# Float16 parts in the key and value product and in most of layer 1's output product, and modulation weights read by half tiles

## The chip, the cores and the metric

The kernel runs on one core of a Trainium2 chip, in one launch. The metric is the device time in microseconds (us), the median of several runs. A measurement is told from no change at about 0.2%.

## What is computed

A two-layer diffusion transformer block stack on 256 image tokens and 256 context tokens of width 2048, with branches 4096 wide. Layer 0 mixes with a Fourier transform, layer 1 with windowed attention that also sees the context; the context itself is only needed as far as layer 1's keys and values. Cut to what matters here:

```python
for i in range(2):
    shift, scale, gate = split(silu(c) @ ada_w[i] + ada_b[i], 3)         # modulation; its own for the context
    h  = rmsnorm(x,  norm_g[i]) * (1 + scale)   + shift
    hc = rmsnorm(xc, norm_g[i]) * (1 + scale_c) + shift_c
    if i == 0:                                   # Fourier branch, image and context
        u, z = split(h @ w_in, 2);  y = mix(fft2(u).real) * silu(z)
    else:                                        # attention branch, image only
        q, k, v, z = split(h @ w_in, [4096, 512, 512, 4096])
        kc, vc     = split(hc @ w_in[:, 4096:5120], 2)
        y = attend_with_sink(rope(q), [rope(k), kc], [v, vc], sink, mask) * silu(z)
    x = x + gate * (y @ w_out[i])                # layer 0: xc too
return rmsnorm(x, final_g)
```

Inputs and outputs are float32.

## The kernel before

Matmuls of float32 accuracy are made of three matmuls on two parts (`mm3`): each operand is cast to a high part on ScalarE (ACT) and the rest is its low part, one subtraction on VectorE (DVE); high x high, high x low and low x high are added up in PSUM. There are two kinds of parts. `half_split` makes fp32r parts (lines 66 and 67). `split16` makes float16 parts (lines 137 and 138); there the operand is scaled first by a power of two that follows from a bound of its size, and the result is scaled back when PSUM is read. Such a bound needs the operand's sum of squares ahead of its first use, so the weights are read once more for it: `scan_loads` brings pieces of w_out of layer 0 (`wo0`), `scan_sums` squares them on ACT with a running sum.

```python
def split16(t, i, up):
    w = wsp.tile([P, 2, 1024], F16, tag="ws", name="wf")
    src = t[:, i * 1024 : (i + 1) * 1024]
    last_cast[0] = S.activation(w[:, 0], src, AF.Copy, scale=up).ins
    last_sub[0] = V.scalar_tensor_tensor(w[:, 1], src, up, w[:, 0], op0=ALU.mult, op1=ALU.subtract).ins
```

Weights arrive as 1 MB tiles on SyncE's queue (SP) into `raw`, three buffers. Their parts lie in `ws`, six buffers of 4 KB per partition: an fp32r half takes two of them (high and low), a float16 half takes one. `act` is a pool of 33 buffers of 2 KB for everything else. PSUM has eight banks, each of 512 float32 columns. Each engine works through its instructions in the order that the program lists them, and this order is a scheduler's, from priorities and the `issue_after` contexts in the code.

The stages that matter, with the times of the profile:

- About 310 to 840 us: layer 0's branch; its z product has float16 parts, and DVE works off "jobs" of modulation beside it (`ada_jobs`): a tile of the modulation weights `adw` is multiplied by silu(c) and summed (line 796).
- About 840 to 1002 us: layer 0's output product `wo0`, 32 steps (two sweeps of 16, `kg`), each 24 matmuls of 512 columns. Float16 parts except in the last two steps of a sweep. Here the modulation jobs go on (`ada_rate` of them in step i), now from 1 MB tiles in `raw`; before this stage they read half tiles, `zr` on SP and `wa` on the queue of GpSimd (POOL), the latter into a `ws` buffer. At the end the residual is taken out of PSUM (`evac0`, line 971).
- About 1002 to 1092 us: the key and value product `wkv`. The normalised, modulated input of layer 1 is made per k tile, 128 features each, as fp32r parts for image (`hx1`) and context (`hc1`) by lines 1107, 1108 and 1111. The loop over 8 weight tiles x 2 k x 4 token blocks x 2 (keys, values) fills all eight PSUM banks; then lines 1132 to 1142 read them (a copy and an absolute value of the values, the rotated keys).
- About 1092 to 1600 us: the products for q and z in units, with attention of 32 head blocks between them, and the first column block of layer 1's output product (`w1_next`, `o1_step`, weights `wo1a`). `hx1` serves q and z too. The attention output `y1` is split by `y_split` into fp32r parts `yh`: k under 16 in buffers "h1", 16 to 23 in "act", 24 to 31 in "ys".
- About 1600 us to the end: the rest of the first column block, then `wo1b` (two column blocks, 16 weight tiles of 2 k, 24 matmuls each) and `wo1c` (the last block), all in fp32r parts with `yh` as the stationary side; `evac` multiplies by the gate (`gbc`) and adds the residual, `finish` normalises and stores.

Of the kernel before, what the change touches and what calls it, by code (L numbers as in the profile page):

```python
# [10 lines left out]
F32 = mybir.dt.float32  # L11
F32R = mybir.dt.float32r
# [5 lines left out]
P = 128  # L18
# [14 lines left out]
def tile_dit(ctx: ExitStack, tc: tile.TileContext, a: dict, out: bass.AP):  # L33
# [591 lines left out]
    def h_bound():  # L625
        m = adap.tile([P, 2], F32, name="hm")
        V.tensor_reduce(m[:, 0:1], gs0.rearrange("p k s -> p (k s)"), axis=AX.X, op=ALU.max, apply_absolute_value=True)
        V.tensor_reduce(m[:, 1:2], sh0.rearrange("p k s -> p (k s)"), axis=AX.X, op=ALU.max, apply_absolute_value=True)
        V.scalar_tensor_tensor(m[:, 0:1], m[:, 0:1], 46.0, m[:, 1:2], op0=ALU.mult, op1=ALU.add)
        return as_b(m[:, 0:1])  # L630
# [8 lines left out]
    for g in range(G):  # L639
# [6 lines left out]
        if g == 13:  # L646
            with tc.issue_after(evacs[g - 2][1]), tc.issue_after(evacs[g - 2][0]):
                hb = h_bound()
# [120 lines left out]
    def ada_jobs():  # L769
        for pieces in ((0,), (1, 2, 3)):  # L770
            for kh in range(2):
# [9 lines left out]
                if True:  # L781
                    for i, fg in order:
                        for f in range(2):
                            q = slice(f * 1024, f * 1024 + 1024)
                            if f == 0 and not out0[0]:
                                wf = adat.tile([P, 1024], F32, tag="zr", name="zr", bufs=2)
                                nc.sync.dma_start(wf, a["adw"][i, kh, fg][:, q])
                            elif not out0[0]:
                                wf = wsp.tile([P, 1024], F32, tag="ws", name="wa")
                                nc.gpsimd.dma_start(wf, a["adw"][i, kh, fg][:, q])  # L790
                            else:
                                if f == 0:
                                    w = raw(a["adw"][i, kh, fg])
                                wf = w[:, q]
# [17 lines left out]
    scans, pend = iter(range(64)), []  # L812

    def scan_sums():
        while pend:
            t, j = pend.pop(0)
            S.activation(t, t, AF.Square, accum_out=scn[:, j : j + 1])

    def scan_loads(n):
        for j in [next(scans) for _ in range(n)]:  # L820
            for q in range(2):
# [3 lines left out]
                pend.append((t, j * 2 + q - 64 * (j >= 40)))  # L825
# [20 lines left out]
    with tc.tile_pool(name="yp", reuse_waits="tile", bufs=32) as ypool:  # L846
# [142 lines left out]
        ada_rate = {**{i: 2 for i in (*range(6, 10), *range(17, 25))}, **{i: 0 for i in (14, 15, 16, 29, 30, 31)}}  # L989
        for i in range(32):  # L990
# [5 lines left out]
            if sw == 0:  # L996
                with tc.issue_after(last_cast[0]):
                    scan_sums()
                scan_loads({6: 1, 7: 1, 8: 1, 9: 1}.get(i, 2) if i < 14 else 0)
# [33 lines left out]

    x1d = dram.tile([2, P, D], F32, name="x1d")
# [46 lines left out]
    def roped(dst, src, tb, pool, tag="rt", eng=V):  # L1081
        t2 = pool.tile([P, 512], F32, tag=tag, name="rt")
        sv = src.rearrange("p (h d) -> p h d", d=64)
        eng.tensor_tensor(dst.rearrange("p (h d) -> p h d", d=64), sv, rope[:, 0, tb, :].unsqueeze(1).broadcast_to([P, 8, 64]), op=ALU.mult)
        s4 = src.rearrange("p (h a t i) -> p h a t i", a=2, t=2, i=16)
        t4 = t2.rearrange("p (h a t i) -> p h a t i", a=2, t=2, i=16)
        sn = rope[:, 1, tb, :].rearrange("p (a t i) -> p a t i", a=2, t=2)
# [4 lines left out]
    with tc.tile_pool(name="h1", reuse_waits="tile", bufs=16) as h1p:  # L1092
# [4 lines left out]
        with tc.tile_pool(name="kvp", reuse_waits="tile", bufs=2) as kvp:  # L1097
            hc1 = []
# [561 lines left out]
```

## Time and profile before

| | |
|---|---|
| median of 3 runs | 1773.9 us (1770.9 to 1774.79) |
| the profiled execution | 1775.4 us |
| its span, first to last instruction | 1773.6 us |
| granted TensorE clock, mean | 0.998 |
| busy: TensorE, DVE, ACT, POOL | 1738.5, 1393.7, 1060.4, 294.8 us |
| moved by DMA | 438.74 MB, 247 GB/s on the mean |

The engines in the profile's lines are PE (TensorE's matmuls), PEld (its weight loads), DVE, ACT, POOL and SP. "L145", "L146" and "L147" are the three matmuls of `mm3`; "L66" and "L67" the two halves of a split; a line out of a helper stands for all its callers, so the tiles' names tell the stage. In a line of instructions, "out<-in" is followed by partitions x elements and type; "x" is the number of them, then busy us and the mean ns of one, then the engine's idle time ahead of them and what ended it. In the timeline the first two columns are start and duration in us. A matmul's own duration there overlaps the next one's, so its pace is read from start to start. In the lines on DMA stand the size and the median time from issue to landing.

### The profile page before, as it was taken

How to read it: one execution, taken by the hardware profiler on the slowest of the kernel's cores; microseconds unless marked ns; L12 is line 12 of the kernel's file. 1: busy time of each engine (PE TensorE's matmuls, PEld its weight loads, DVE VectorE, ACT ScalarE, POOL GpSimd, SP SyncE). 2: the span in 40 equal slices, each digit the busy share in tenths (PEclk: the TensorE clock that was granted, in tenths of full speed). 3: DMA queues.
4: the chain of work that ended last, by engine and by line, in shares of the span. 5: the costliest groups of instructions: out<-in, count | busy, mean ns of one | idle time of the engine just before them, and what ended most of it. 6: DMA issues, size and time to landing. Idle time of an engine off the chain costs nothing.

```text
span 1773.6 us, 26403 instructions
## 1 busy us (share of the span) xinstructions
PE 1738.5 (98%) x9517; PEld 1221.7 (69%) x9517; DVE 1393.7 (79%) x2401; ACT 1060.4 (60%) x1989; POOL 294.8 (17%) x368
## 2 busy tenths in 40 slices
PE   6999999999999999999999999999999999999997
PEld 4679999644444444446444888788888888887886
DVE  5779888797777788876885744899999999996455
ACT  5545556477777745553122534787888888885343
POOL 0002111212222132000000000412302230233010
PEclk9999999999999999999999999999999999999999
DMA  9998999778998889865775323588888888887543
GB/s 393 417 346 252 282 264 262 291 285 318 329 306 316 314 293 349 324 249 181 288 297 187 120 95 119 166 207 200 223 205 211 214 214 211 208 212 248 191 166 143
DMA packets 220962, 438.74 MB, mean 247 GB/s; under 512 B 154720, under 2 KB 155120, under 8 KB 189088
## 3 DMA queue, kind: packets, MB, share of 16 engines
q1 hardware_dynamic: 182784, 351.85, 60.6%
q0 software_dynamic: 33904, 78.25, 14.8%
q10 hardware_dynamic: 4144, 6.95, 1.2%
q8 instruction: 75, 1.23, 0.3%
q14 instruction: 55, 0.45, 0.1%
HBM read 391.91 MB, written 12.59 MB: 228 GB/s over the span
## 4 chain that ended last, share of the span: by engine, by line
PE 90%; DVE 4%; DMA 3%; ACT 2%; issue 1%; POOL 0%; ACTq 0%; POOLq 0%; SPq 0%; DVEq 0%
PE ps L145 24%; PE ps L147 24%; PE ps L146 24%; PE ps L1324 6%; PE ps L1326 3%; PE ps L1395 1%; PE ps L1360 1%; PE ps L1361 1%; PE ps L1396 1%; DMA ft<-f 1%; PE ps L286 1%; DMA raw<-in_awp 1%; DVE wl L67 1%; ACT act L864 0%; ACT wf L137 0%
## 5 line engine op out<-in xcount | busy, mean ns | idle before, releaser
L67 DVE TENSOR_TENSOR wl<-raw,wh 128x1024 fp32r<-128x1024 f32 x213 | 281.1, 1324 | 145.5 <-ACT wh L66 129.2
L66 ACT CAST wh<-raw 128x1024 fp32r<-128x1024 f32 x213 | 222.4, 1045 | 178.4 <-PE ps L146 149.7
L146 PE MATMUL ps<-act,wf 128*128 128x512 f16 x512 | 194.0, 379 | 0.0
L147 PE MATMUL ps<-act,wf 128*128 128x512 f16 x512 | 191.1, 379 | 0.0
L145 PE MATMUL ps<-act,wf 128*128 128x512 f16 x512 | 189.8, 379 | 0.6 <-ACT wf L137 0.3
L1324 PE MATMUL ps<-h,wh 128*128 128x512 f32 x512 | 184.8, 396 | 0.0
L147 PEld LDWEIGHTS <-wf 128*128 128x128 f16 x960 | 93.9, 98 | 113.3
L145 PEld LDWEIGHTS <-wf 128*128 128x128 f16 x960 | 93.7, 98 | 113.4 <-ACT wf L137 4.3
L145 PE MATMUL ps<-y,wf 128*128 128x512 f16 x448 | 169.5, 379 | 0.9 <-ACT wf L137 0.9
L146 PE MATMUL ps<-y,wf 128*128 128x512 f16 x448 | 169.8, 379 | 0.0
L146 PEld LDWEIGHTS <-wf 128*128 128x128 f16 x960 | 93.9, 98 | 109.0
L147 PE MATMUL ps<-y,wf 128*128 128x512 f16 x448 | 165.6, 379 | 0.0
L137 ACT ACTIVATE wf<-raw,nrm 128x1024 f16<-128x1024 f32 x56 | 61.2, 1140 | 153.2 <-DMA raw<-in_wo 131.4
L1326 PE MATMUL ps<-h,wl 128*128 128x256 f32 x512 | 138.6, 281 | 0.0
L146 PE MATMUL ps<-wl,h 128*128 128x512 f32 x320 | 126.7, 396 | 0.0
L147 PE MATMUL ps<-wh,h 128*128 128x512 f32 x320 | 125.3, 395 | 0.0
L145 PE MATMUL ps<-wh,h 128*128 128x512 f32 x320 | 124.0, 402 | 0.0
L1378 DVE SCALAR_TENSOR_TENSOR f<-p,sm,f 128x512 f16<-128x512 f32 x128 | 107.4, 859 | 8.6 <-ACT f L1377 8.3
L138 DVE SCALAR_TENSOR_TENSOR wf<-raw,tn,wf 128x1024 f16<-128x1024 f32 x64 | 79.8, 1282 | 42.6 <-ACT wf L137 42.6
L1365 ACT ACTIVATE p<-ps,mx 128x512 f32<-128x512 f32 x128 | 87.9, 688 | 37.2 <-DVE mx L1362 30.8
L1324 PEld LDWEIGHTS ps<-h,wh 128*128 128x128 f32 x512 | 96.2, 188 | 18.9
L1377 ACT ACTIVATE f<-p,sm 128x512 f16<-128x512 f32 x128 | 87.6, 717 | 31.6 <-DMA ft<-f 12.5
(394 smaller groups left out, 4450.2 us busy)
## 6 DMA issues: line engine op xcount, KB each, us to landing
raw<-in_wz SPq DMA_DIRECT2D x64, 1024.0 KB, 5.5
raw<-in_adw SPq DMA_DIRECT2D x38, 1024.0 KB, 6.0
raw<-in_awp SPq DMA_DIRECT2D x32, 1024.0 KB, 13.1
act<-in_wo POOLq DMA_DIRECT2D x128, 256.0 KB, 7.4
raw<-in_wo SPq DMA_DIRECT2D x32, 1024.0 KB, 6.6
raw<-in_wq SPq DMA_DIRECT2D x32, 1024.0 KB, 5.1
raw<-in_wu SPq DMA_DIRECT2D x32, 1016.0 KB, 6.9
raw<-in_wo1b SPq DMA_DIRECT2D x16, 1024.0 KB, 4.9
```

Source lines behind the costliest of these rows:

```text
L66: last_cast[0] = S.copy(h, src).ins
L67: last_sub[0] = eng.tensor_tensor(l, src, h.bitcast(F32), op=ALU.subtract).ins
L137: last_cast[0] = S.activation(w[:, 0], src, AF.Copy, scale=up).ins
L138: last_sub[0] = V.scalar_tensor_tensor(w[:, 1], src, up, w[:, 0], op0=ALU.mult, op1=ALU.subtract).ins
L145: PE.matmul(o, wh, xh, start=start, stop=False)
L146: PE.matmul(o, wh, xl, start=False, stop=False)
L147: return PE.matmul(o, wl, xh, start=False, stop=stop).ins
L1324: PE.matmul(o[0], wh[:, q], hx1[k], start=k == 0, stop=k == KT - 1)
L1326: PE.matmul(o[0][:, 0:N], wl[:, q], hx1[k][:, 0:N], start=False, stop=False)
L1365: S.activation(pt[tb], so[tb], AF.Exp, bias=mx[:, tb : tb + 1], scale=-1.0, accum_out=sm[:, tb : tb + 1])
L1377: S.activation(f[:, 0:512], pt[tb], AF.Copy, scale=sm[:, tb : tb + 1])
L1378: V.scalar_tensor_tensor(f[:, 512:1024], pt[tb], sm[:, tb : tb + 1], f[:, 0:512], op0=ALU.mult, op1=ALU.subtract)
```

## The change

- **Key and value product.** Weights and input become float16 parts. The input is made as scaled float16 parts `hz` (lines 1156, 1158 and 1160 of the changed kernel); since q and z still want fp32r parts, `make_hx1` makes these once more for the image, beside the product (lines 1190 to 1192). Keys and values are scaled back as PSUM is read: the rotation uses a scaled table `ropek`, other copies take a scale.
- **The scales.** `h1_bound` and `h1_scale` work out the input's and the weights' scale at the end of `wo0`, with one trip through DRAM (`hbd`) that brings all partitions' values to each. The sums of squares come from a scan over `wkv`, 14 tiles of `wo1b` and 7 of `wo1c`: 22 half pieces as 44 tiles of 256 KB in steps 10 to 29 of `wo0` (`scan_loads1`, `w_rate`, ACT's squares in line 829), 36 half pieces of 512 KB during the key and value product (`loads2`, line 1184, four buffers `pz`; `sums2`, 28 squares on ACT in line 1177, 8 on DVE in line 1179).
- **Layer 1's output product.** In 28 of 32 k steps of `wo1b` and `wo1c` both sides are float16 parts; `y_sums` squares the attention output on ACT during attention, `out_scale` makes the scales at its end, `y_half` makes y's float16 parts, and `gbc` carries the scale back. The last four k stay fp32r, with scaled weights (`w_scaled`). `wo1a` stays fp32r; `y_split` puts k under 24 in "h1" buffers.
- **Modulation.** The jobs in `wo0` read half tiles (`zr` and `wa`) as the earlier ones do, and `ada_rate` changes in steps 25 and 28.

The core of the diff:

```diff
-                            if f == 0 and not out0[0]:
+                            if f == 0:
                                 wf = adat.tile([P, 1024], F32, tag="zr", name="zr", bufs=2)
                                 nc.sync.dma_start(wf, a["adw"][i, kh, fg][:, q])
-                            elif not out0[0]:
+                            else:
                                 wf = wsp.tile([P, 1024], F32, tag="ws", name="wa")
                                 nc.gpsimd.dma_start(wf, a["adw"][i, kh, fg][:, q])
...
+    def scan_loads1(n):
+        for j in [next(scans1) for _ in range(n)]:
+            for q in range(2):
+                t = act()
+                c = (j % 2 * 2 + q) * 512
+                nc.gpsimd.dma_start(t, wst[j // 2][:, c : c + 512])
...
-        ada_rate = {**{i: 2 for i in (*range(6, 10), *range(17, 25))}, **{i: 0 for i in (14, 15, 16, 29, 30, 31)}}
+        ada_rate = {**{i: 2 for i in (*range(6, 10), *range(17, 26))}, **{i: 0 for i in (14, 15, 16, 28, 29, 30, 31)}}
+        w_rate = {**{i: 1 for i in (10, 14, *range(17, 26), 29)}, **{i: 2 for i in (15, 16, 26, 27, 28)}}
+        def h1_bound():
+            m, c = h_bound(gs1, sh1, False), tiny(F32, 4, "t4")
...
+            nc.gpsimd.dma_start(hbd, c[:, 0:2])
+            hb1.append(act())
+            nc.gpsimd.dma_start(hb1[0][:, 0:N], hbd.rearrange("(o p) c -> o (p c)", o=1).broadcast_to([P, N]))
...
             elif i == 31:
+                with tc.issue_after(last_sub[0]):
+                    h1_scale()
                 wr = raw(a["wkv"][0])
-                w0 = half_split(wr, 0)
+                w0 = split16(wr, 0, upk)
+            if i == 28:
+                with tc.issue_after(last_sub[0]):
+                    h1_bound()
...
+                    h, l = (z2[:, s * 512 + c : s * 512 + c + N] for c in (0, N))
+                    V.scalar_tensor_tensor(t[:, q], x1[k][:, q], gsz[:, k, s : s + 1], r_bc1[:, q] if k else r_ps[s], op0=ALU.mult, op1=ALU.mult)
+                        a_ = S.activation(h, t[:, q], AF.Identity, bias=shz[:, k, s : s + 1]).ins
+                        e = V.scalar_tensor_tensor(l, t[:, q], shz[:, k, s : s + 1], h, op0=ALU.add, op1=ALU.subtract).ins
...
+            def sums2(act_only):
+                for n in range(len(pend)):
+                    t, c = pend.pop(0)
+                    if n % 5 < 3 or act_only:
+                        S.activation(t, t, AF.Square, accum_out=c)
+                    else:
+                        V.tensor_tensor_reduce(t, t, t, 1.0, 0.0, ALU.mult, ALU.add, c)
+            def loads2(n):
+                for j in [next(scans1) for _ in range(n)]:
+                    t = kvp.tile([P, 1024], F32, tag="pz", name="pz", bufs=4)
+                    nc.gpsimd.dma_start(t, wst[j // 2][:, j % 2 * 1024 : j % 2 * 1024 + 1024])
+            def make_hx1(k):
+                V.scalar_tensor_tensor(t, x1[k][:, 0:N], gs1[:, k, 0:1], r_bc1[:, 0:N], op0=ALU.mult, op1=ALU.mult)
+                S.activation(hx[:, 0:N], t, AF.Identity, bias=sh1[:, k, 0:1])
+                V.scalar_tensor_tensor(hx[:, N : 2 * N], t, sh1[:, k, 0:1], hx[:, 0:N].bitcast(F32), op0=ALU.add, op1=ALU.subtract)
...
             for kg in range(8):
-                    w = ws_split(raw(a["wkv"][kg])) if kg else [w0, half_split(wr, 1)]
+                    w = [split16(wr, i, upk) if kg or i else w0 for i in range(2)]
+                with tc.issue_after(last_cast[0]), tc.issue_after(ends[min(kg * 4 + 3, 15)][0]):
+                    sums2(kg < 3)
+                with tc.issue_after(pow_end[0]):
+                    loads2((6, 6, 6, 6, 6, 6, 0, 0)[kg])
...
+                    for k in range(kg * 3 - 3, min(kg * 3, KT)) if kg else ():
+                        make_hx1(k)
...
-                            mm3(o[tb][kv], h[:, c : c + P], h[:, N + c : N + c + P], wh[:, q], wl[:, q], k == 0, k == KT - 1)
+                            mm3(o[tb][kv], hz[k][:, c : c + P], hz[k][:, N + c : N + c + P], wh[:, q], wl[:, q], k == 0, k == KT - 1)
...
+            def y_sums(n, i):
+                    S.activation(act(), y1[j], AF.Square, accum_out=yq[:, j : j + 1])
+            def y_half(j):
+                t = h1p.tile([P, 1024], F16, tag="h1", name="yf", bufs=16)
+                S.activation(t[:, 0:512], y1[j], AF.Copy, scale=uy)
+                V.scalar_tensor_tensor(t[:, 512:1024], y1[j], uy, t[:, 0:512], op0=ALU.mult, op1=ALU.subtract)
...
+            S.activation(gbc[:, 512:], gbc[:, 512:], AF.Copy, scale=dn1)
...
-                w = ws_split(raw(a["wo1b"][kg]))
+                t = raw(a["wo1b"][kg])
+                w = [split16(t, i, uw) if kg < 14 else w_scaled(t, i) for i in range(2)]
+                if kg + 3 < 14:
+                        y_half(kg + 3)
...
-                            mm3(o[tb][c], yh[k][:, tb * P : (tb + 1) * P], yh[k][:, N + tb * P : N + (tb + 1) * P], wh[:, q], wl[:, q], k == 0, k == NB - 1)
+                            mm3(o[tb][c], *(t[:, tb * P : (tb + 1) * P] for t in y_parts(k)), wh[:, q], wl[:, q], k == 0, k == NB - 1)
```

More of the change, by code (lines that the diff above doesn't have):

```diff
@@ L1031, in tile_dit @@
                     evac0(sw * 8 + b, o[b])
+    V.tensor_reduce(yq[:, 16:17], scn[:, 4:16], axis=AX.X, op=ALU.add)
     x1d = dram.tile([2, P, D], F32, name="x1d")
@@ L1448, in tile_dit, with x2_load @@
             nc.gpsimd.dma_start(gbc, gated.broadcast_to([P, D]))
-            x2 = []
-            for tb in range(2):
-                x2.append([act() for _ in range(4)])
-                for c in range(4):
+            x2 = [[], []]
+            def x2_load(c):
+                for tb in range(2):
+                    x2[tb].append(act())
                     nc.gpsimd.dma_start(x2[tb][c], x1d[tb, :, c * 512 : (c + 1) * 512])
+            x2_load(0)
             fg = fp.tile([P, D], F32, name="fg")
```

160 lines of the change are left out of this document (117 added, 43 removed).

## Prediction

> **What bounds the kernel now.** I read the page first, for the shares and the chain.
>
> ```profile
> span 1773.6 us, 26403 instructions
> PE 1738.5 (98%) x9517; PEld 1221.7 (69%) x9517; DVE 1393.7 (79%) x2401; ACT 1060.4 (60%) x1989; POOL 294.8 (17%) x368
> PE 90%; DVE 4%; DMA 3%; ACT 2%; issue 1%; POOL 0%; ACTq 0%; POOLq 0%; SPq 0%; DVEq 0%
> ```
>
> TensorE (PE) is busy 98% of the span and carries 90% of the chain that ended last. So what counts is how many matmuls there are and how far apart they start, not what the other engines do, as long as they keep up. Next came the table by windows, for the stages that the change touches: the output product of layer 0 (842 to 975), the key and value product (1020 to 1064), attention (1140, 1550) and the output product of layer 1 (1641 to 1729).
>
> ```profile
> core 0: us, PE busy (x) PEld busy (x) DVE busy (x) ACT busy (x) POOL busy (x), PEclk, DMA share, GB/s
> 842.46:887.00 44.54, 44.54 (x208) 20.16 (x207) 38.44 (x60) 8.76 (x8) 0.00 (x0) 1.00 0.76 289
> 887.00:931.00 44.00, 44.00 (x205) 19.95 (x204) 39.14 (x59) 9.49 (x9) 0.00 (x0) 1.00 0.77 296
> 1020.00:1064.00 44.00, 44.00 (x190) 35.44 (x189) 21.64 (x39) 14.27 (x25) 0.00 (x0) 1.00 0.27 96
> 1140.00:1186.00 46.00, 43.86 (x246) 36.85 (x245) 42.28 (x75) 38.16 (x76) 14.68 (x10) 1.00 0.75 186
> 1550.00:1596.00 46.00, 46.00 (x245) 37.76 (x244) 44.23 (x82) 40.93 (x90) 16.28 (x16) 1.00 0.82 215
> 1641.00:1685.00 44.00, 44.00 (x192) 35.63 (x191) 19.04 (x17) 16.84 (x16) 0.00 (x0) 1.00 0.55 191
> 1685.00:1729.00 44.00, 44.00 (x191) 35.61 (x190) 25.44 (x24) 19.08 (x24) 4.77 (x3) 1.00 0.48 167
> ```
>
> PE is full at the whole granted clock in the products, while VectorE (DVE) and ScalarE (ACT) are half idle in the key and value product (21.64 and 14.27 of 44 us) and at the end. They are nearly full in attention (DVE 44.23 of 46). Last I read PE's own timeline and the chain, for the pace of one matmul.
>
> ```profile
> 1013.40 0.40 PE L145 MATMUL ps<-wh,h 128*128 128x512 f32 x1
> ...
> 1015.97 0.40 PE L147 MATMUL ps<-wh,h 128*128 128x512 f32 x1
> 839.35 0.38 PE L147 MATMUL ps<-y,wf 128*128 128x512 f16 x1
> ...
> 841.94 0.38 PE L147 MATMUL ps<-y,wf 128*128 128x512 f16 x1
> ```
>
> ```profile
> 1630.83 0.93 PE ps L145 x4
> 1633.63 0.93 PE ps L145 x4
> ...
> 1675.63 0.91 PE ps L145 x4
> 1678.35 0.91 PE ps L145 x4
> ```
>
> Key and value product, fp32r parts: 11 steps in 2.57 us, 233.6 ns apart. Layer 0's output product, float16 parts: 12 steps in 2.59 us, 215.8 ns. The chain through layer 1's output product shows one k step of 12 matmuls each 2.80 us (233.3 ns) and, further on, each 2.72 us (226.7 ns); the second pace goes with the eight steps k = 16 to 23 whose attention parts lie in "act" buffers. So fp32r costs 11 to 18 ns more for each matmul. The weight loads differ in the same sense:
>
> ```profile
> L146 PEld LDWEIGHTS ps<-wl,ys 128*128 128x128 f32 x192 | 36.1, 188 | 8.5 <-DVE wl L67 0.2
> L147 PEld LDWEIGHTS <-wf 128*128 128x128 f16 x960 | 93.9, 98 | 113.3
> ```
>
> The Trainium skill (TensorE: Matmul & The Clock Gate, "Wait — 56ns, not 53.3ns?") gives a warm 512-column matmul 215.7 ns from start to start, whatever the type. By that rule the change removes nothing from PE. The float16 rows agree with it (215.8); the fp32r rows do not (233.6), and the measurement decides.
>
> **What the change removes.** Key and value product: 16 k x 4 token blocks x 2 halves x 3 = 384 matmuls x (233.6 - 215.8) = 6.8 us. Layer 1's second and third column blocks: 28 of 32 steps, 12 and 6 matmuls each, 18 together. Twenty of those steps run at 233.3 now: 20 x 18 x 17.5 = 6.3 us; eight at 226.7: 8 x 18 x 10.9 = 1.6 us. The first column block stays fp32r, and its eight "act" steps move to the "h1" buffers: 8 x 6 x 6.6 ns = 0.3 us lost, if the pace goes with the buffer. Sum: 6.8 + 6.3 + 1.6 - 0.3 = **14.4 us**. PE is full there, so this counts one to one if the feeding keeps up.
>
> **What it adds, and where that lies.** Prices:
>
> ```profile
> L645 ACT ACTIVATE pz<-pz 128x1024 f32<-128x1024 f32 x12 | 12.8, 1065 | 5.5 <-DMA pz<-in_wz 5.5
> L817 ACT ACTIVATE act<-act 128x512 f32<-128x512 f32 x128 | 78.6, 615 | 0.0
> L817 ACT ACTIVATION_READ_ACCUMULATOR act<-act 128x1 f32 x128 | 24.0, 188 | 0.0
> L796 DVE CUSTOM_DVE_ANT_0 wa<-wa,cb 128x1024 f32<-128x1024 f32 x26 | 31.8, 1223 | 0.7
> L1107 DVE SCALAR_TENSOR_TENSOR ht<-act,gs 128x256 f32<-128x256 f32 x30 | 12.7, 479 | 0.3 <-ACT act L1113 0.3
> L1108 ACT ACTIVATE h<-ht,sh 128x256 fp32r<-128x256 f32 x16 | 8.1, 507 | 7.5 <-DVE ht L1107 7.4
> L883 DVE SCALAR_TENSOR_TENSOR y<-y,nrm 128x512 f16<-128x512 f32 x28 | 19.9, 748 | 5.9 <-ACT y L882 5.9
> wa<-in_adw POOLq DMA_DIRECT2D x26, 512.0 KB, 5.3
> pz<-in_wz SPq DMA_DIRECT2D x12, 512.0 KB, 6.3
> act<-in_wo POOLq DMA_DIRECT2D x128, 256.0 KB, 7.4
> gated<-gr POOLq DMA_DIRECT2D x1, 8.0 KB, 3.3
> ```
>
> *Layer 0's output product.* 44 quarter pieces (256 KB) are loaded and squared on ACT: 44 x (615 + 188) = 35 us, where ACT has 8.76 of 44.54 us to do; 11.5 MB more over 200 us adds 58 GB/s to 289 GB/s. Modulation does the same number of reductions from half tiles; DVE is 38 to 39 of 44 us busy and stays so. The half tiles wait for a buffer of the weights' parts, hence for PE, on GpSimd's queue (POOL), and the scan's loads queue behind them. The bound calculation's trip through memory is a write and a read of about 3.3 us each, while one k step of this stage is 24 matmuls, 5.2 us; its scalars stand between i = 31's last subtraction and the first float16 cast of the key weights, where PE still has that step's 5.2 us and the residual's evacuation to run. I take 0.7 us here, between 0 and 3.
>
> *Key and value product.* ACT gets 28 squares (30 us) and 16 copies (8 us), DVE 8 squares (10 us) and 32 instructions of the attention input made again (15 us). In 82.9 us ACT has about 65 and DVE about 70 us of work, so neither becomes the bound on the mean. The 36 half pieces (18.9 MB) add about 240 GB/s to 96 for some 80 us; the opening of the same run moves 393 to 417 GB/s, so the bytes fit:
>
> ```profile
> GB/s 393 417 346 252 282 264 262 291 285 318 329 306 316 314 293 349 324 249 181 288 297 187 120 95 119 166 207 200 223 205 211 214 214 211 208 212 248 191 166 143
> ```
>
> The order is what can hurt. POOL's loads in the changed kernel, at the head of this product (pz is the buffer of a half piece that the scan squares):
>
> ```order
> L1110 DMA gated<-gr 16x128 [waits DMASW4_49,Activation_49]
> L1184 DMA pz<-in_wo1b 128x1024 [waits DMASW5_49]
> L1184 DMA pz<-in_wo1b 128x1024 [waits DMAHW2_49,DMAHW6_49,DMASW6_49,Pool_49]
> L1184 DMA pz<-in_wo1b 128x1024 [waits DMAHW5_49,DMAHW1_49,DMASW7_49]
> L1184 DMA pz<-in_wo1b 128x1024 [waits DMASW0_49]
> L1184 DMA pz<-in_wo1b 128x1024 [waits DMASW1_49,Activation_49]
> L1184 DMA pz<-in_wo1b 128x1024 [waits DMASW2_49,Activation_49]
> ```
>
> Four loads go out at once; from the fifth on, each waits for a square to free its buffer. And ACT's queue at the end of the product, before:
>
> ```order
> L66 CAST wh<-raw 128x1024 [waits DMAHW4_49,DVE_49,PE_49]
> L66 CAST wh<-raw 128x1024 [waits DVE_49,PE_49]
> L66 CAST wh<-raw 128x1024 [waits DMAHW5_49,DVE_49,PE_49]
> L66 CAST wh<-raw 128x1024 [waits DVE_49,PE_49]
> L1135 COPY act<-ps 128x512 [waits PE_49]
> L1136 ACTIVATE act<-ps 128x512
> ```
>
> and after:
>
> ```order
> L66 CAST wh<-raw 128x1024 [waits PE_49]
> L1177 ACTIVATE pz,scn<-pz 128x1024 [waits DMASW7_49,Activation_49]
> L1177 ACTIVATE pz,scn<-pz 128x1024 [waits DMASW2_49,Activation_49]
> L1177 ACTIVATE pz,scn<-pz 128x1024 [waits DMASW3_49,Activation_49]
> L1177 ACTIVATE pz,scn<-pz 128x1024 [waits DMASW4_49,DVE_49]
> L1177 ACTIVATE pz,scn<-pz 128x1024 [waits DMASW5_49,DVE_49]
> L66 CAST wh<-raw 128x1024 [waits PE_49]
> L1223 COPY act<-ps 128x512 [waits PE_49]
> L1224 ACTIVATE act<-ps 128x512
> ```
>
> Before, ACT has only weight casts ahead of the evacuation (L1135, now L1223). Now five squares, each with a wait for its own load, stand right ahead of it, and PE's next products need the banks that it empties.
>
> ```profile
> 1002.13 0.48 PE L145 MATMUL ps<-wh,h 128*128 128x512 f32 x1
> 1026.74 0.49 ACT L1108 ACTIVATE h1c<-ht,sh 128x256 fp32r<-128x256 f32 x1
> 1087.80 0.59 ACT L1135 COPY act<-ps 128x512 f32<-128x512 f32 x1 [0.58 <-PE ps L147]
> 1091.80 0.40 PE L1147 MATMUL ps<-act,oner 128*128 128x512 f32 x1
> ```
>
> The first four squares stand behind 24 of 32 parts of the input, which before were made by 1027. The evacuation would begin at 1087.8 - 6.7 = 1081.1, and 29 of 36 loads are taken ahead of it: with four buffers, seven rounds after the first, so (1081.1 - 1028) / 7 = 7.6 us for a round. A round is a landing, a square of 1.07 us, and a wait in ACT's queue, about 0.7 us (an estimate: two squares of three stand right behind another, 2/3 x 1.07): 5.3 + 1.8 = 7.1 us by the nearest row (same size, same queue), 6.3 + 1.8 = 8.1 by the next, 7.4 + 1.8 = 9.2 by the farthest. The first costs nothing; the second is 7 x 0.5 = 3.5 us late; the third 11.2. The first token block's banks are full three blocks (3 x 1.3 = 3.9 us) before the product's end and take two copies, 2 x 0.59 = 1.2 us, to empty, so 2.7 us of lateness is hidden. Cost: 0, 0.8 or 8.5 us. I take **1.5**, near the first two, with two squares of DVE among the rotations behind it.
>
> *Attention.* 14 squares of the attention output on ACT, 14 x 0.8 = 11 us over 460 us, where ACT has 38 to 41 of 46 us to do and DVE 42 to 44. PE is full, so most of it is covered; without that cover all 11 count, and the evenly spread square is on the softmax's way once in 33 us. I take 0.5, between 0 and 3.
>
> *Layer 1's output product.* Splitting y costs about 0.7 us on ACT (an estimate, between L817's 615 and L883's 748 ns) and 0.75 on DVE (L883) for a pair of k, under a PE step of 5.18 us where DVE has 19 of 44 us to do; the scale's chain is a dozen tiny operations at i = 64, while PE still runs attention's last blocks; gbc's scaling stands ahead of ACT's first cast of wo1b. I take 0.3, between 0 and 2.
>
> Sum: -14.4 + 0.7 + 1.5 + 0.5 + 0.3 = **-11.4 us**. The profiled execution took 1775.4 us (span 1773.6 and 1.8 around it), 1.5 above the median of the runs shown, 1773.9. 1775.4 - 11.4 = 1764.0, less those 1.5: **1762.5 us**. By the skill's rule of one pace for all types the sum would be +3.0 instead, 1776.9.
>
> **The rivals.** *(a) The covers are thinner than the busy shares say.* Layer 0's output product and attention have DVE over 85% and 92% busy, and what ACT adds to their order delays a cast now and then. At the upper bounds of the two (3 + 3) and of the end (2) the loss is 9.5 instead of 3.0: 1769. For it: DVE's 44.23 of 46. Against: PE shows no gap at 842 to 931, with the reductions already as dense.
>
> *(b) Slower: the scan's loads hold ACT at the end of the key and value product.* Place: the five squares ahead of L1223. Each round over 7.6 us counts seven times, less 2.7. The gain of 14.4 less 1.5 elsewhere is gone at a round of 7.6 + (12.9 + 2.7) / 7 = 9.8 us; at 10.4 the time is about 1778. It needs a landing of 8 us and more; the rows have 5.3 to 7.4, the latter at 289 GB/s and more, and this stage would run at about 336. Casts held in the same queue would add to it. The Trainium skill (DMA: Bandwidth & Descriptors, "Queues, rings and completion order") says that each DMA engine takes turns between queues by the packet, so these loads and the weights' on SP slow each other; no row of before shows this mix.
>
> *(c) Float16 doesn't run at 215.8 ns here*, since before has no float16 matmul with these tiles as the stationary side, or half of the gap comes from buffers, as the 226.7 shows: half the gain, 7.2 - 3.0, gives 1769.7; none gives 1776.9.
>
> **How the numbers follow.** Forecast 0.60 (1759.5 to 1766), better than that 0.05 (every cost zero: 1759.5, and a stall of before gone besides), (a) 0.17, (b) 0.08 for slower and 0.04 for about even, (c) 0.06, half of it slower or even. The range, 1757.5 to 1771, takes in the first three. A measurement of this kernel tells 0.2%, 3.5 us, from no change. Faster: 0.60 + 0.05 + 0.15 + 0.02 = 0.82; slower 0.10; same 0.08.
>
> **What would show it.** Right: in the profile after, float16 matmuls 216 ns apart at 1002 to 1085, the product ending about 6.8 us sooner, PE's windows there and at the end still full, L1223 beginning within 3 us of its first bank. Wrong: an idle time on PE released by ACT or DVE behind L1223 or L1132 (b), idle of PE released by L137, L138 or the softmax (a), a pace of 226 ns or more (c).

## Result and profile after

The changed kernel took 1784.86 us (median of 4 runs, 1782.87 to 1787.67) against 1772.4 us of the kernel before (4 runs): ratio 1.0069, 95% interval 1.0052 to 1.0087. It is slower by 0.7%, clear of the noise. Measured again later beside other kernels (e12 below) it took 1786.9 against 1775.91, ratio 1.0046 (1.0026 to 1.0066). The predicted 1762.5 and its range up to 1771 were wrong.

The page of the changed kernel, and its windows in the stages shown of before and at the end of the key and value product:

```profile
span 1781.1 us, 26884 instructions
PE 1730.6 (97%) x9523; PEld 1145.4 (64%) x9523; DVE 1430.2 (80%) x2492; ACT 1146.5 (64%) x2192; POOL 362.7 (20%) x488
```

```profile
core 0: us, PE busy (x) PEld busy (x) DVE busy (x) ACT busy (x) POOL busy (x), PEclk, DMA share, GB/s
842.46:887.00 44.54, 44.54 (x209) 20.15 (x207) 28.60 (x41) 11.72 (x19) 15.02 (x28) 1.00 1.03 390
1020.00:1064.00 44.00, 44.00 (x206) 19.93 (x204) 36.98 (x71) 39.83 (x75) 10.56 (x20) 1.00 0.87 321
1085.00:1096.00 11.00, 2.43 (x10) 1.31 (x8) 3.99 (x8) 5.82 (x12) 1.05 (x2) 0.72 0.79 298
1550.00:1596.00 46.00, 45.24 (x249) 37.37 (x248) 43.24 (x80) 41.54 (x97) 22.44 (x23) 1.00 0.76 195
1653.00:1697.00 44.00, 44.00 (x205) 19.95 (x204) 31.20 (x28) 25.08 (x28) 3.36 (x2) 1.00 0.63 217
```

PE is full in both products, and more matmuls fit into the same 44 us (206 records against 190 at 1020, 205 against 192 in the output product). But 8.6 of 11 us stand empty at 1085 to 1096, just where the key and value product ends. DMA is now busy 0.87 of the time in that product, at 321 GB/s, where before had 0.27 at 96. PE's timeline in the product and at its end:

```profile
1012.98 0.38 PE L145 MATMUL ps<-wf,hz 128*128 128x512 f16 x1
1013.20 0.38 PE L146 MATMUL ps<-wf,hz 128*128 128x512 f16 x1
...
1085.93 0.38 PE L147 MATMUL ps<-wf,hz 128*128 128x512 f16 x1
1094.88 0.79 PE L1235 MATMUL ps<-act,oner 128*128 128x512 f32 x1 [8.57 <-DVE scn L1179]
1095.47 0.63 PE L145 MATMUL ps<-wh,h 128*128 128x512 f32 x1
1095.90 0.63 PE L146 MATMUL ps<-wl,h 128*128 128x512 f32 x1
```

The float16 pace is the forecast 216 ns, and the product takes 82.7 us (1003.27 to 1085.93) instead of 89.7. Then PE waits 8.57 us, and the matmuls after that start 0.43 us apart for some 4 us. The Trainium skill (TensorE: Matmul & The Clock Gate, "What's actually happening") says that idle PE falls back to half the clock; a 512-column matmul then takes 426.7 ns by that page, and the rows agree with it.

Where the time went, by stretches of the PE timeline (us):

| from, to | before | after | after again (e12) | forecast |
|---|---|---|---|---|
| start to last float16 matmul of layer 0's output product | 971.4 | 971.2 | 971.9 | +0.7 with the next |
| to first matmul of the key and value product | 30.7 | 32.1 | 37.3 | |
| to the matmul on the absolute values (L1147, now L1235) | 89.7 | 91.6 | 92.7 | -6.8 and +1.5 with the next |
| to the first matmul of z's low part | 56.2 | 59.0 | 58.5 | |
| to the last one of z | 419.3 | 422.8 | 422.3 | +0.5 |
| to PE's last matmul | 196.9 | 195.4 | 195.2 | -7.3 |

So about 12 us were lost at the end of the key and value product, 3 in attention, 6 of the output product's saving at the end of attention, and 1 to 7 ahead of the key and value product.

In all of these places but attention PE's clock has a part in it: behind some of PE's waits, in some executions, the windows show a granted clock of 0.50 for several us. What it cost can be estimated by adding up, over windows of 2 us, PE's busy time times what the granted clock lacks of 1. This gives 1.5 us in the profile before (at 1611 to 1617), 6.0 in the changed kernel's (2.6 behind the gap at the product's end, 3.4 at 1618 to 1627) and 10.6 in e12 (5.1 ahead of the key and value product, 2.1 behind the gap, 3.4 at 1625 to 1633).

### The profile page after: what moved, and what is told of

The parts are those of the page before. It is cut to its first block, busy times and chain, and to the rows that moved or that the text cites. A ratio compares the mean times of both kernels' runs of the same rounds, so it can differ in the third digit from the quotient of the medians.

```text
span 1781.1 us, 26884 instructions
## 1 busy us (share of the span) xinstructions
PE 1730.6 (97%) x9523; PEld 1145.4 (64%) x9523; DVE 1430.2 (80%) x2492; ACT 1146.5 (64%) x2192; POOL 362.7 (20%) x488
## 5 line engine op out<-in xcount | busy, mean ns | idle before, releaser
L67 DVE TENSOR_TENSOR wl<-raw,wh 128x1024 fp32r<-128x1024 f32 x152 | 203.3, 1340 | 28.2 <-ACT wh L66 27.4
L66 ACT CAST wh<-raw 128x1024 fp32r<-128x1024 f32 x152 | 158.2, 1041 | 37.2 <-PE ps L146 24.1
L829 ACT ACTIVATE act<-act 128x512 f32<-128x512 f32 x172 | 105.8, 616 | 14.8 <-DMA act<-in_wo1b 9.0
L138 DVE SCALAR_TENSOR_TENSOR wf<-raw,tn,wf 128x1024 f16<-128x1024 f32 x64 | 79.8, 1282 | 42.5 <-ACT wf L137 42.4
L790 POOL DMA_DIRECT2D wa<-in_adw x64 | 34.0, 532 | 385.9 <-DVE acc L792 131.0
L1504 DVE SCALAR_TENSOR_TENSOR f<-p,sm,f 128x512 f16<-128x512 f32 x128 | 102.8, 827 | 11.4 <-ACT f L1503 11.2
L146 PE MATMUL ps<-wl,h 128*128 128x512 f32 x256 | 102.8, 402 | 0.6 <-DVE wl L67 0.6
## 6 DMA issues: line engine op xcount, KB each, us to landing
raw<-in_awp SPq DMA_DIRECT2D x32, 1024.0 KB, 12.7
```

Of the source, the lines that this page charges most:

```text
L66: last_cast[0] = S.copy(h, src).ins
L67: last_sub[0] = eng.tensor_tensor(l, src, h.bitcast(F32), op=ALU.subtract).ins
L146: PE.matmul(o, wh, xl, start=False, stop=False)
L829: S.activation(t, t, AF.Square, accum_out=c)
L1504: V.scalar_tensor_tensor(f[:, 512:1024], pt[tb], sm[:, tb : tb + 1], f[:, 0:512], op0=ALU.mult, op1=ALU.subtract)
```

## Experiments

All ratios are against the kernel before on the same chip, which took between 1772.1 and 1775.9 us there. A profile shows one execution only, and those of one kernel spread, up to 1769.7 to 1788.7 us (e2): the profiles of e1 (1768.84 us) and e6 (1767.21) lie near the lower end of their kernel's spread, those of e7 (1775.86) and e11 (1774.13) near the upper end. What a profile shows need not hold for every execution behind the median.

**Is the gap at the product's end the scan? (e1, e6, e4.)** ACT's timeline in the changed kernel ahead of the evacuation, a square on DVE at the same place, and the DMA rows of the scan:

```profile
1084.29 1.06 ACT L1177 ACTIVATE pz<-pz 128x1024 f32<-128x1024 f32 x1 [0.66 <-DMA pz<-in_wo1c]
1087.12 1.06 ACT L1177 ACTIVATE pz<-pz 128x1024 f32<-128x1024 f32 x1 [1.68 <-DMA pz<-in_wo1c]
1091.77 1.06 ACT L1177 ACTIVATE pz<-pz 128x1024 f32<-128x1024 f32 x1 [3.50 <-DMA pz<-in_wo1c]
1092.82 1.03 ACT L66 CAST wh<-raw 128x1024 fp32r<-128x1024 f32 x1
1093.76 0.57 ACT L1223 COPY act<-ps 128x512 f32<-128x512 f32 x1
1093.65 1.23 DVE L1179 CUSTOM_DVE_ANT_0 pz<-pz 128x1024 f32<-128x1024 f32 x1 [7.01 <-DMA pz<-in_wo1c]
```

```profile
pz<-in_wo1b POOLq DMA_DIRECT2D x22, 512.0 KB, 6.8
pz<-in_wo1c POOLq DMA_DIRECT2D x14, 512.0 KB, 7.0
raw<-in_wkv SPq DMA_DIRECT2D x8, 1024.0 KB, 6.6
```

The evacuation (L1223) began at 1093.76, 12.7 us after the forecast 1081.1, behind squares that waited for their loads. PE's row above names DVE's square, which had waited 7.01 us for its own load and ended at 1094.88; the values that the matmul reads come from ACT's L1224, which ended just before it, at 1094.83. So both engines stood behind the same stream of loads. e1 takes the loads and squares out:

```diff
-                    loads2((6, 6, 6, 6, 6, 6, 0, 0)[kg])
+                    pass
```

> Leaves out the 36 half-piece loads and their squares beside the key and value product (the layer 1 output weights' sum is then that of the first 14 half pieces alone). Theory one, ACT's evacuation is held by squares that wait for their loads: PE's gap of 8.95 us behind the product's last matmul and the slow clock behind it (some 2.5 us) go, L1223 begins near 1082 instead of 1093.8, the time falls by 11 to 12 us to about 1773.5. Rival, the input made a second time and the float16 casts overload ACT and DVE: the gap stays above 5 us and the time falls by less than 5.

Measured: 1776.19 us, ratio 1.0008 (0.9992 to 1.0025). The gap is gone (the matmul on the absolute values starts at 1085.16, 0.03 us after the last of the product), and z begins at 1142.3 instead of 1153.9. e6 keeps every instruction and halves the bytes (the squares read the loaded half twice):

```diff
-                    nc.gpsimd.dma_start(t, wst[j // 2][:, j % 2 * 1024 : j % 2 * 1024 + 1024])
+                    nc.gpsimd.dma_start(t[:, 0:512], wst[j // 2][:, j % 2 * 1024 : j % 2 * 1024 + 512])
```

> The changed kernel with half of the bytes in each of the 36 loads beside the key and value product (256 KB instead of 512; the squares stay as long, over the same half twice, so the scan's sums are other ones). Theory one, the landing sets the rounds: landing falls from 6.9 to 4 or 5 us, eight rounds fit, L1223 begins by 1084, the gap is under 1 us, about 1774 to 1777. Rival, ACT's and DVE's own work and order (all instructions are still there): the gap stays over 5 us, 1783 and above.

Measured: 1776.46 us, ratio 1.0009 (0.9988 to 1.0029). Its scan rows and PE at the product's end:

```profile
pz<-in_wo1b POOLq DMA_DIRECT2D x21, 256.0 KB, 4.8
pz<-in_wo1c POOLq DMA_DIRECT2D x14, 256.0 KB, 4.1
1085.52 0.51 PE L1237 MATMUL ps<-act,oner 128*128 128x512 f32 x1 [0.55 <-ACT act L1226]
```

With a landing of 4.1 to 4.8 us the same instructions in the same order cost 0.55 us in this execution. So it is the landing behind which ACT stands, not ACT's and DVE's own work. e4 keeps all bytes and squares and moves 12 of 36 behind the evacuation:

```diff
-                    loads2((6, 6, 6, 6, 6, 6, 0, 0)[kg])
+                    loads2((6, 6, 6, 6, 0, 0, 0, 0)[kg])
...
+            for _ in range(3):
+                loads2(4)
+                with tc.issue_after(kr_end):
+                    sums2(True)
```

> The same scan, all of it, but 24 of the 36 half pieces go beside the key and value product and 12 are squared on ACT behind the evacuation of its banks. Theory one: the gap at the product's end goes, the 12 squares (13 us of ACT) lie beside the q product where ACT has 27 of 44 us to do, and cost 0 to 2 us; 1773 to 1776. Rival, bytes of the scan slow the weights' own loads wherever they lie: a gap of some us moves behind the evacuation and the time stays above 1779.

Measured: 1781.66 us, ratio 1.0033 (1.0014 to 1.0052). The gap is gone here too (1084.78), but PE then waits 4.4 us for casts at 1090 to 1125 (its waits name DVE's L67), so part of the loss moved behind the evacuation, as the rival had it. The median is above the expectation, and 6.7 us above this profile's execution (1774.92); what the others lost no profile shows.

**Attention and its end (e2, e3, e7).** e2 leaves out the 14 squares of the attention output (`y_sums`), e3 puts the y parts of k = 16 to 23 back into act buffers, e7 is e1 and e2 together.

```diff
-                    S.activation(act(), y1[j], AF.Square, accum_out=yq[:, j : j + 1])
+                    pass
```

> Leaves out the 14 squares of the attention output on ACT during attention (a constant stands for their sum). The changed kernel loses 3.5 us between the first and the last z matmul and 6.2 more from there to the output product. Theory A, the squares in ACT's queue delay the softmax and the casts: 4 to 9 us of that come back, about 1776 to 1781. Theory B, the y parts of k = 16 to 23 wait for h1 buffers and the squares are covered: less than 1.5 us, about 1784.

```diff
+                if 16 <= k < 24:
+                    t = act(F32R)
...
```

> The changed kernel with the y parts of k = 16 to 23 in act buffers again, as before the change. Theory B (these parts wait for h1 buffers that the first steps still read, and the end of attention is late for it): 4 to 6 us come back, about 1779 to 1781; also the eight steps run at 227 instead of 233 ns, 0.3 us. Theory A (the squares): within 1 us of the changed kernel's 1784.9.

> The changed kernel without the 36 loads and squares beside the key and value product and without the 14 squares of the attention output, both left out. If the two losses add up: 1784.9 less 9 less 4 to 7, 1768 to 1772. If the end of attention is late for another reason (order of y's splits, transposes by DMA): as e1, about 1775.

Measured: e2 1781.08 (ratio 1.0034, 1.0008 to 1.0059), e3 1787.23 (1.0074, 1.0051 to 1.0096), e7 1768.93 (0.9972, 0.9951 to 0.9993). z's low-part matmuls, their number and first and last start, of before, after, e2 and e7:

```profile
L1326 PE MATMUL ps<-h,wl x512: 277/282/282, 1148.0 to 1567.3; 128*128 128x256 f32 x171
L1450 PE MATMUL ps<-h,wl x512: 277/282/384, 1153.9 to 1576.7; 128*128 128x256 f32 x171
L1450 PE MATMUL ps<-h,wl x512: 277/282/282, 1161.6 to 1581.9; 128*128 128x256 f32 x171
L1450 PE MATMUL ps<-h,wl x512: 277/282/282, 1152.5 to 1572.8; 128*128 128x256 f32 x171
```

419.3, 422.8, 420.3 and 420.3 us. Over all profiles of this study the eight with the squares have 421.5 to 425.0 us (mean 422.9), the nine without 419.1 to 420.9 (mean 420.0): the squares cost 2.9 us in this stretch. Which instructions they delay is not shown: in the changed kernel's profile PE waits 0.40 us at 1426.6 for DVE's L67, for example, but the cast that this L67 reads stood ahead of the nearest square. e3 gained nothing: theory B falls. The times of e2 and e3 hold the gap at the product's end as well (8.7 and 8.8 us in their profiles), so the stretch, not the time, tells.

From the last z matmul to the end e2 takes 189.5 us, but e7 still 192.0, where 189.6 was due (196.9 less 7.3). There the profile of e7 shows PE waiting for DMA transposes of the softmax. Transposes on SP and the loads of residual and gate on POOL, of before and after:

```profile
1594.58 2.61 SPq L1380 DMA_TRANSPOSE ft<-f  x2
1602.59 4.35 POOL L1453 DMA_DIRECT2D act<-x1d  x8
1609.69 0.56 POOL L1448 DMA_DIRECT2D gbc<-gated  x1
```

```profile
1598.83 1.12 POOL L1583 DMA_DIRECT2D act<-x1d  x2
1600.99 5.94 SPq L1506 DMA_TRANSPOSE ft<-f  x2
1607.99 5.09 SPq L1506 DMA_TRANSPOSE ft<-f  x2
1611.27 0.54 POOL L1577 DMA_DIRECT2D gbc<-gated  x1 [11.32 <-PE ps L1487]
```

Before, the residual's pieces and the gate's load leave 8 and 15 us after the last transposes began. After, two residual pieces leave 2 us ahead of a pair of transposes, and the gate's load 3 us into the next pair, with the final gain and four more pieces right behind; these pairs take 5 to 6 us to issue instead of 2.6. That the loads alone do it is not shown: in e3 they leave only at 1626 to 1632, and a pair at 1600.15 takes 5.06 us all the same.

**Late loads at attention's end (e14).** e7, the sink operations moved (below), and the gate's load made to wait for a value of the last unit that is transposed by DMA; the other loads follow it.

```diff
+                if i == 61:
+                    V.tensor_copy(yq[:, 30:31], ob[:, 0:1])
...
-            nc.gpsimd.dma_start(gbc, gated.broadcast_to([P, D]))
+            V.tensor_copy(gbc[:, 0:1], yq[:, 30:31])
+            gbc_i = nc.gpsimd.dma_start(gbc, gated.broadcast_to([P, D])).ins
...
```

> As e7 (no loads and squares beside the key and value product, no squares of y) with the sink operations moved, and the gate's, the residual's and the final gain's loads wait for the last unit of attention that is transposed by DMA. From the last z matmul to the end e7 took 192.0 us and before 196.9, where 7.6 less was expected. If those loads slow the last two transposes (4.6 to 8 us instead of 3.4): the stall ahead of the last value product goes under 2 us and this stretch takes 188 to 190. Rival, the weights' loads or the softmax's order: 191 to 193 as in e7.

Measured: 1760.66 us (1759.05 to 1762.23), ratio 0.9932 (0.9915 to 0.995).

```profile
1592.83 2.62 SPq L1507 DMA_TRANSPOSE ft<-f  x2
1614.66 0.57 POOL L1581 DMA_DIRECT2D gbc<-gated  x1 [30.12 <-issue]
```

The last transposes take 2.62 us again, and the stretch from the last z matmul to the end 186.7 us, about 10 less than before and more than expected. This stretch differs between executions by PE's clock. Less the estimate for it, it takes 186.7 us in e14 and 189.0 in e15 below, both with the late loads; 189.5 to 192.9 (mean 191.5) in the ten other profiles with the changed output product; 193.7 to 195.4 (mean 194.5) in the five with the output product of before. So the late loads are worth some 2 to 5 us, and the changed output product without them gave 3 of the 7.3 forecast.

**Ahead of the key and value product (e5, e8, e10, e9, e11, e13).** e5 is the key and value part alone, with modulation's half tiles and the scan of the key and value weights; e8 also moves DVE's two operations on the sink values behind the float16 parts of the input; e10 is the kernel before with the half tiles alone.

```diff
-    V.tensor_scalar(nsink, sink, -1.0, None, op0=ALU.mult)
...
+            with tc.issue_after(ends[15][1]):
+                V.tensor_scalar(nsink, sink, -1.0, None, op0=ALU.mult)
```

> Only the key and value product's part of the change and modulation's half tiles: layer 1's output product is as before, the scan covers the key and value weights alone (16 half pieces during layer 0's output product), nothing is scanned beside the key and value product, and no squares of y. If the sum's first term holds (6.8 us) and the output part's scan and squares are all that was lost: no gap at the product's end, attention as before, and 1767 to 1769 beside 1775 of before. Rival, the head start (scale and sink loads ahead of the residual's end) and the second making of the input cost as much as the product gains: 1773 and above.

> As e5, and DVE's two operations on the sink values stand behind the input's float16 parts instead of inside the residual's evacuation, where they waited up to 2.0 us for the sink's load. If that wait is on the path to the key and value product: 0.5 to 3 us less than e5. If it is covered: the same within 0.5.

> The kernel before with modulation's half tiles during layer 0's output product as the only change. Theory: PE gaps at 900 to 960 in some executions, 1 to 4 us slower than before. Rival: no difference within 1 us, since without the scan POOL's queue is free.

Measured: e5 1772.8 us (ratio 0.9996, 0.998 to 1.0011), e8 1774.39 (0.9997, 0.9987 to 1.0007), e10 1773.55 (0.9991, 0.998 to 1.0002). Neither half tiles alone (as the rival had it) nor the key and value part with them moves the median; e5 lies above what was expected, and e8 gains nothing on it. The profile of e8 shows where the saving went: waits at 900 to 950 us, as engine, line, what it waited for, us in total, times, longest.

```profile
DVE junk L792 <- DMA zr<-in_adw: 6.4, 3, 2.7
PE ps L147 <- DVE wf L138: 4.1, 3, 3.0
```

A reduction on DVE waits for its half tile, the making of the weights' low float16 part (L138) stands behind it, and PE behind that. In e9 modulation reads 1 MB tiles again:

```diff
-                            if f == 0:
+                            if f == 0 and not out0[0]:
...
-                            else:
+                            elif not out0[0]:
                                 wf = wsp.tile([P, 1024], F32, tag="ws", name="wa")
                                 nc.gpsimd.dma_start(wf, a["adw"][i, kh, fg][:, q])
+                            else:
+                                if f == 0:
+                                    w = raw(a["adw"][i, kh, fg])
+                                wf = w[:, q]
```

> As e8 (key and value product alone, sink operations moved), and modulation reads 1 MB tiles during layer 0's output product again, as before the change. Theory, the half tiles hold the weights' parts buffers and POOL's queue there and lose 0 to 5 us from run to run: no PE gap over 0.3 us at 900 to 960, a median of 1767 to 1769 against 1775 of before. Rival, the scan's own loads do it: gaps of 0.5 to 5 us stay, 1772 to 1774 as e5 and e8.

Measured: 1769.6 us (1766.64 to 1771.6), ratio 0.9958 (0.9944 to 0.9972), no PE gap over 0.3 us there. It leaves out no part of the computation and is 6.3 us faster than the kernel before, about the forecast saving of this product alone. e11 is e7 with these 1 MB tiles and the sink operations moved:

> The changed kernel with the four suspects out at once: no loads and squares beside the key and value product, no squares of y (both left out), 1 MB modulation tiles, sink operations moved. If these four are all that eats the saving on PE: 1775 less 14.4 plus 1 to 3, 1762 to 1764. If something else does too: above 1767.

Measured: 1770.94 us, ratio 0.9966 (0.9955 to 0.9978), above the expectation. Its profile has the saving from the key and value product on (781.1 us from the last float16 matmul of layer 0's output product to the end, 792.7 before, so 11.6 less), but its branch of layer 0 ended 3 us late, and that output product had five gaps of 0.95 to 1.85 us between starts at 860 to 940, 6.9 together, where PE waits for ACT's casts. So in this execution, with the longer scan, the 1 MB tiles cost time, while with the shorter scan the half tiles did; the medians of e11 and e7 do not tell the two kinds apart. Why the gaps begin at 860, where both scans are still the same, is open. e13 moves only the sink operations in the changed kernel:

> The changed kernel with DVE's two operations on the sink values behind the input's float16 parts, nothing else. From the last float16 matmul of layer 0's output product to the first of the key and value product before has 30.7 us; the changed kernel had 32.1 in its first profile and 37.4 in its second, and the kernels with the sink operations moved 30.9 to 31.0. If the sink's load, late on POOL's queue, is what lengthens it: 31 us here too and a time 1 to 7 us under the unaltered kernel's 1786, 1779 to 1785. If the scan's late reduction (line 1081) is: 35 us and more in some profiles, no change of the time.

Measured: 1782.99 us, ratio 1.0061 (1.0037 to 1.0086). The time is within the expectation for the sink's load, but the stretch ahead of the key and value product is 32.4 us, as in the changed kernel's first profile (32.1). The waits of e13 at 970 to 1004 us name another cause beside it:

```profile
DVE adab L1081 <- ACT act L829: 10.8, 1, 10.8
ACT act L829 <- DMA act<-in_wo1b: 9.9, 1, 9.9
```

The reduction of the scan's first part (L1081) stands on DVE ahead of the last weight splits and waits 10.8 us for a square of a piece loaded late. Why the piece is late stands in POOL's queue, here of the changed kernel's first profile:

```profile
963.88 0.55 POOL L1013 DMA_DIRECT2D hbd<-tn  x1 [21.95 <-DVE tn L1009]
968.21 0.54 POOL L1015 DMA_DIRECT2D act<-hbd  x1 [3.78 <-DMA hbd<-tn]
969.79 1.07 POOL L821 DMA_DIRECT2D act<-in_wo1b  x2
```

The bound's write (`hbd`) waits 21.95 us for its value and its read 3.78 us for the write to land, and the scan's last piece stands behind both. The profiles together show how the reduction and the sink's load add up. Where the reduction began up to 6.0 us after the last float16 matmul (e1, e4, e6), the stretch took 31.2 us; at 6.8 us (the first profile), 32.1. Where it began 7.7 to 9.2 us after it, the stretch took 37.3 to 40.1 us with the sink operations in place, whose wait of 0.8 to 2.0 us came on top (e2, e3, e7, e12), and 31.9 and 32.4 us with them moved (e14, e13). The step between is PE's clock, by these windows of e12 and e13:

```profile
1000.00:1005.00 5.00, 5.00 (x26) 5.00 (x26) 1.27 (x7) 2.96 (x6) 1.74 (x3) 0.50 0.00 0
995.00:1000.00 5.00, 4.81 (x41) 4.54 (x41) 1.59 (x7) 2.65 (x7) 0.25 (x1) 1.00 0.01 2
```

In e12 PE had waited 2.14 us for DVE's L991, and the granted clock was then 0.50 for some 10 us; in e13 it had waited 1.43 us there and kept its whole clock.

**The changed kernel again, and a mended one (e12, e15).**

> The changed kernel unaltered, beside the others on the same chip, for its spread and a second profile. 1782 to 1788; the gap at the end of the key and value product 8 to 10 us again; gaps at 925 to 945 and at 992 that differ from the first profile's.

e12: 1786.9 us (1775.6 to 1789.24); its gap at the end of the key and value product is 10.1 us, and the stretch ahead of it 37.3 us. Seven of its nine executions lie at 1785 and above, at a mean granted clock of 0.991 to 0.993, and two at 1775.6 and 1776.5, at 0.998 and 0.997. No profile is of such an execution, so whether the gap comes in all of them is open. e15 keeps all of the change's computation; the last half piece of the scan and 12 others lie behind the evacuation, the sink operations and the late loads are moved as above.

```diff
-        w_rate = {**{i: 1 for i in (10, 14, *range(17, 26), 29)}, **{i: 2 for i in (15, 16, 26, 27, 28)}}
+        w_rate = {**{i: 1 for i in (10, 14, *range(17, 26))}, **{i: 2 for i in (15, 16, 26, 27, 28)}}
...
+            for n_ in (4, 4, 5):
+                loads2(n_)
```

> All of the change's computation, with the order mended in four places: 13 of 37 half pieces of the scan are squared behind the evacuation (as e4), the last half piece during layer 0's output product moves to them, the sink operations stand behind the input's parts, and the gate's, residual's and final gain's loads wait for the last unit transposed by DMA (as e14). From e14's 1760.7: plus 3.5 to 5 for the squares of y, plus 2 to 3 for the late squares, less about 1 for the reduction that waited: 1765 to 1769, under the 1772 to 1776 of before and level with e9's 0.9958. If the order was not what cost: above 1775.

Measured: 1769.69 us (1767.37 to 1773.48), ratio 0.9973 (0.9961 to 0.9984), just above the expectation. The stretch ahead of the product is 31.3 us, and the product's end has no gap. The late squares still cost PE 3.3 us at 1090 to 1125, and attention takes 422.2 us with y's squares. So order alone, with all the work kept, turns a loss of 11 to 12 us into a gain of about 6.

## Why the prediction was wrong

- **The saving on PE: right.** The key and value product took 82.7 instead of 89.7 us (forecast 6.8 less), the output product ran at 216 ns, and e14, with two pieces of ACT's work left out and the order mended, reached 1760.7 beside 1772.1, 11.4 less. That this is just the forecast's sum is luck, since e14's end of attention gained more than was forecast. The pace by the Trainium skill (TensorE: Matmul & The Clock Gate, "Wait — 56ns, not 53.3ns?"), whose formula has only the number of columns in it, does not hold for all of these rows: only float16 ran at 216 ns.
- **The end of the key and value product: the step that failed.** 1.5 us was taken, about 12 came (8.95 of gap, and 2.8 on the way to z, 2.6 of it PE's slow clock by the estimate above). The place, the mechanism and the formula were those of rival (b), which had a chance of 0.08. Its inputs were wrong twice. The landing was taken between 5.3 and 6.3 us from stages with other traffic, on the ground that the bytes fit under the opening's GB/s; it was 6.8 to 7.0 at a DMA share of 0.87, and the weights' own tiles went from 4.8 to 6.6. That agrees with the Trainium skill (DMA: Bandwidth & Descriptors, "Queues, rings and completion order"), by which the queues take turns on each DMA engine. And the count was wrong: 33 of 36 squares stand ahead of L1223, not 29, so eight rounds of 8.8 us (1021.4 to 1091.8) instead of seven, where 7.5 were allowed ((1081.1 - 1021.4) / 8). The slow clock behind such a gap was not priced at all.
- **Attention: 0.5 taken, 2.9 to 3.5 measured.** The free time of ACT was read as cover, and with the squares left out the stretch is 2.9 us shorter. That is what rival (a) said of this stage; by which delayed instruction, no run shows.
- **The output product's stretch: 7.3 less forecast, 1.5 came.** The weights' and y's casts did hide, as said (PE 44.00 of 44.00 at 1653). What was missed lies at the end of attention: the loads of gate, gain and residual on POOL's queue, which cost some 2 to 5 us (e14 and e15 against the rest), and PE's slow clock behind the waits there, 3.4 us in this profile and 1.5 before.
- **Layer 0's output product and behind it: 0.7 taken, 1.1 in the first profile and 7.1 in the second.** The bound's trip through memory was covered for the first float16 cast, as said, but not for POOL's queue: the scan's last piece stood behind it, and the reduction L1081 behind that piece (10.8 us on DVE), which the prediction did not list. To this came the sink's load, PE's clock of 0.50 behind the two in e12, and, in some executions, the half tiles. The scan's loads also came denser than the 58 GB/s that were added: 842 to 887 us moved 390 GB/s where 289 were before, though PE stayed full. (The product begins at 659 us in the profile before and not at about 840, and each of its 32 steps is 48 matmuls, 10.4 us; 5.2 us is one k.)

## What to carry to other kernels

A faster matmul is only worth what the work that it needs leaves of it, and that work is to be placed by the order of each engine's queue, not by its busy share: a square that waits for its own load must not stand ahead of the evacuation that PE waits for. Price a stream of loads by the landing under the traffic that it makes itself, and count its rounds from the order. A wait of PE can cost more than its length: look at the granted clock behind it, too. Where a load moves on a queue, look for the short transfers of other queues that it will meet.

## What the runs showed of the hardware

The 512 KB loads landed in 6.8 to 7.0 us and the 256 KB ones in 4.1 to 4.8 us in the same place, so half the bytes saved a third of the time and the gap with it. DMA transposes took 5.1 to 5.9 us to issue in pairs late in the changed kernel's attention, and 2.6 in e14 with the late loads; what lengthened them is in part open (e3). A gap of 9 us on PE cost some 2.6 us more behind it, at 426 to 427 ns from start to start. A wait of 2.1 us ahead of the key and value product was followed by some 10 us at a granted clock of 0.50 (e12), where waits of 1.0 to 1.4 us at the same place left it at 1.00 (e14, the first profile, e13).
